# Weight additions and row scaling of a second feed-forward product moved from GpSimd to VectorE

## The chip, the cores and the metric

The kernel runs on one core of a Trainium2 chip. The metric is the device time of one execution in microseconds (us). The core has five engines that each work through their own list of instructions in the order written: TensorE (matrix products; PE in the profile, its weight loads PEld), VectorE (DVE), ScalarE (ACT), GpSimd (POOL) and SyncE (SP), which here only issues transfers. They wait for one another through semaphores.

## The reference

One layer of a decoder for 2048 tokens of width 1024, in fp32. Around the part that matters here:

```python
h = h + jnp.einsum('bsm,md->bsd', mixed, w_out[l])       # after the two mixers
nm = rmsnorm(h, mlp_norm_g[l])
a = jnp.square(jax.nn.relu(jnp.einsum('bsd,df->bsf', nm, w_ff1[l])))   # width 4096
h = h + jnp.einsum('bsf,fd->bsd', a, w_ff2[l])
...
return rmsnorm(h, final_norm_g)
```

The change lies in the last product, `a` (2048 x 4096) by `w_ff2` (4096 x 1024), and in the final norm, which divides each token's row by its root mean square and multiplies it by a vector of 1024 factors.

## The kernel before

Everything is fp32; a product of two fp32 matrices is made of three matmuls on rounded parts. Each operand is split into a high part (a rounded copy, made by ScalarE) and a low part (the operand less its high part, made by VectorE), and `mm3` (L132 to L134) adds high by high, low by high and high by low in PSUM.

The second feed-forward product isn't done block by block. Each half of the tokens (1024) has four blocks of 256 rows, the inner width of 4096 is cut into four, the 1024 output columns into two. Instead of 4 x 4 x 2 = 32 block products a half, the kernel does 26 products of combinations: sums and differences of activation blocks by sums and differences of weight blocks, each result added to or subtracted from some of the eight output sums of a half. The table `PRODUCTS` lists for each product which combination of activations it takes, its sign, whether it begins a new accumulation in PSUM, and which output sums take it (numbered l = 2m + n, row block m and column half n). The combinations of activations were formed and stored to memory during the first feed-forward product. The combinations of weights are formed on the way: three raw buffers of 1024 x 512 (each in two halves of 128x2048) hold them, and the table `WEIGHTS` says for each of 24 weights for how many products it serves, in which buffer it lies, what is loaded into which buffer, and the one addition or subtraction of two buffers that makes it. The lists `first_of` and `weight_of` turn this into product numbers. `tD` is a combination kept in memory.

Time is counted in steps: 26 products, each for two halves (a phase, `ph`), each phase of 8 steps, and in a step six matmuls (one chunk of 128 of the inner width, for two groups of 128 tokens, three matmuls each): 416 steps. The order of every engine's instructions is written out by hand: `at_step(n, f, ...)` puts an instruction into the list of step n, and `step(n)` issues that list, in the order in which it was filled, before the matmuls of step n. What belongs to the change's surroundings, for a weight whose first product begins at step `at`:

- `load_t` (L1664, SP's queue): the raw weight halves, at steps at - 22 and at - 16
- `add_t` (L1672): the addition, a quarter (128x1024) at a time, at steps at - 16, - 13, - 9 and - 6
- `hi_t` (L1684, ScalarE) and `lo_t` (L1688, VectorE): the two parts of each quarter (tile `ct`), between steps at - 11 and at - 1
- for the activations of a phase: `load_s` (L1633, SP), `hi_s` (L1646, ScalarE) and `lo_s` (L1651, or L1653 for a product of negative sign; VectorE; tile `cs`), 6 to 1 steps ahead of their use
- `taken` (L1737, VectorE): in the first two steps behind a phase, adds the finished PSUM results to the output sums (tiles `sum` and `acc`)

When an output sum has its last product, `taken` calls `output` for each group of 128 rows: `square` (ScalarE, L1708) sums the squares of the 512 columns; where the row's other half is already complete, `root` (VectorE L1714 and L163, then the power on GpSimd, L164) makes the row's factor, `scale` multiplies both halves by it and by the final norm's factors `gF`, and `store` (L1722, L1723, SP's queue) writes them. These are 1, 2, 4 and 6 steps behind; for the last sum (half 1, l = 3) they follow at once. Of a row's two column halves, the second (`C[1]`) is scaled by one VectorE instruction (L1718). The first (`C[0]`) is multiplied by `gF` on GpSimd (L1710) as soon as its sum is complete and squared, and later by the row's factor on ScalarE (L1719).

Weights 17 to 23 of the table begin at products 19 to 25, so at steps 304 to 400; all of them but weight 19 (steps 336 to 351) have an addition, which is made within the 16 steps before the weight's first step.

Of the kernel before, what the change touches and what calls it, by code (L numbers as in the profile page):

```python
# [13 lines left out]
AF = mybir.ActivationFunctionType  # L14
OP = mybir.AluOpType
# [91 lines left out]
def emit(tc, a, stop=99):  # L107
    nc = tc.nc
    V, A, G, T, SP = nc.vector, nc.scalar, nc.gpsimd, nc.tensor, nc.sync
# [44 lines left out]
    def stat(n=1):  # L154
        if stat_at[0] + n > 96:
            stat_at[0] = 0
        s = stats[:, stat_at[0]:stat_at[0] + n]
        stat_at[0] += n
        return s

    def rstd_of(ssq, width, n=1, X=V):
        r, r2 = stat(n), stat(n)
        X.tensor_scalar(r, ssq, 1.0 / width, EPS, op0=OP.mult, op1=OP.add)  # L163
        G.tensor_tensor(r2, r, mhalf[:, :n], op=OP.pow)  # L164
        return r2
# [82 lines left out]
    C = {(0, 0): c11, (0, 1): c12, (1, 0): c21, (1, 1): c22}  # L248
# [309 lines left out]

    R, PV = {}, {}

    def square(key, src, junk):
        R[key] = stat()
        A.activation(junk, src, AF.Square, accum_out=R[key])

    def root(key):
        R[key] = rstd_of(R[key], D)

    def scale(key, src, cs=slice(0, D)):
        V.scalar_tensor_tensor(src[:, cs], src[:, cs], R[key], gB[:, cs], op0=OP.mult, op1=OP.mult)

# [21 lines left out]
    def spread_roots(k):  # L592

        rows[k] = ps("d")
        for i in range(4):
            T.matmul(rows[k][:, 128 * i:128 * i + 128], R[8 + 4 * k + i].to_broadcast([128, 128]), ident,
                     start=True, stop=True)
# [146 lines left out]
    with tc.manual_schedule(engines={X.engine for X in (T, V, A, G, SP)}):  # L744
# [79 lines left out]
        for t in range(3, 8):  # L824
            n = t + 1
# [23 lines left out]
        for t in range(12, base[NG] + 10):  # L849
# [7 lines left out]
            if T0 <= t < base[NG]:  # L857
                g = max(g for g in range(NG) if base[g] <= t)
                x, i = divmod(t - base[g], length[g])
# [426 lines left out]
    for pr in range(4):  # L1286
# [3 lines left out]
        for hh, br in seq:  # L1290
            b = Branch()
            b.h, b.br = 2 * pr + hh, br
            m = 4 if br == 2 else 2
# [66 lines left out]
    gM, gF = gs[:, :D], gs[:, D:2 * D]  # L1360
# [215 lines left out]
    for at, t in enumerate(tiles):  # L1576
        u, m = nxt
# [37 lines left out]
    first_of, weight_of = [], []  # L1615
# [39 lines left out]
    def traw(b, h):  # L1655
        if (b, h) not in raw_t:
            raw_t[b, h] = view(acc1[2 + h] if b == 2 else slot("rt"), (4, 512))
        return raw_t[b, h]
# [7 lines left out]
    def add_t(q, u):  # L1666

        _, _, _, add, stored = WEIGHTS[q]
        if add is not None:
            d, x, op, y = add  # L1670
            d, x, y = [traw(b, u // 2)[:, u % 2 * 2:u % 2 * 2 + 2] for b in (d, x, y)]
            G.tensor_tensor(d, x, y, op=OP.add if op == "+" else OP.subtract)  # L1672
            if stored:
                at_step(now[0] + 4, SP.dma_start, tD[:, 2 * u:2 * u + 2], d)

# [21 lines left out]
    def output(half, l, i):  # L1697

        m, n = divmod(l, 2)
        scr = gM[:, 512 * (i % 2):512 * (i % 2) + 512]  # L1700
        C = [sums[half, m][:, i, 512 * k:512 * k + 512] for k in range(2)]
        col = 16 * half + 4 * m + 2 * i
        at_end = last_at[l] > last_at[2 * m + 1 - n]
        row = 1024 * half + 256 * m + i * 128
        R = []

        def square():
            A.activation(scr, C[n], AF.Square, accum_out=oss[:, col + n:col + n + 1])  # L1708
            if n == 0:
                G.tensor_tensor(C[0], C[0], gF[:, :512], op=OP.mult)  # L1710

        def root():
            s1 = stat()
            V.tensor_tensor(s1, oss[:, col:col + 1], oss[:, col + 1:col + 2], op=OP.add)  # L1714
            R.append(rstd_of(s1, D))

        def scale():
            V.scalar_tensor_tensor(C[1], C[1], R[0], gF[:, 512:], op0=OP.mult, op1=OP.mult)  # L1718
            A.activation(C[0], C[0], AF.Copy, scale=R[0])  # L1719

        def store():
            SP.dma_start(out2[row:row + 128, 512:], C[1])  # L1722
            (A if (half, l, i) == (1, 3, 1) else SP).dma_start(out2[row:row + 128, :512], C[0])  # L1723

        for n_, f in zip((1, 2, 4, 6), (square, root, scale, store) if at_end else (square,)):
            if (half, l) == (1, 3):
                f()
            else:
                at_step(now[0] + n_, f)

    def taken(ph, i, p):

        k, half = divmod(ph, 2)
        for l, sign in PRODUCTS[k][3]:
            m, n = divmod(l, 2)
            c = sums[half, m][:, i, 512 * n:512 * n + 512]
            V.tensor_tensor(c, c, p, op=OP.add if sign > 0 else OP.subtract)  # L1737
            if last_at[l] == k:
                output(half, l, i)
# [8 lines left out]
    steps, now = {}, [0]  # L1748
# [8 lines left out]
    def at_step(n, f, *args):  # L1757
        steps.setdefault(n, []).append((f, args))
# [6 lines left out]
    for ph in range(2 * NR):  # L1765
        for u, n in ((0, -6), (1, -3)):
            n = 4 if (ph, u) == (1, 1) else 8 * ph + n
# [4 lines left out]
    for q, at in enumerate(first_of):  # L1772
        at *= 16
        for h, n in ((0, -22), (1, -16)):
            at_step(max(at + n, -4 + 3 * h) if q else -18 + h, load_t, q, h)
        for u in range(4):
            at_step(at + (-16, -13, -9, -6)[u], add_t, q, u)
        for u in range(4):
            n = at + ((-11, -8, -4, -2) if q else (-10, -8, -5, -2))[u]
            at_step(n, hi_t, q, u)  # L1780
            at_step(n + 1, lo_t, q, u)
# [21 lines left out]
    with tc.manual_schedule(engines={X.engine for X in (T, V, A, G, SP)}):  # L1803
# [16 lines left out]
        for at in range(7, len(jobs1)):  # L1820
# [3 lines left out]
            m = parts_at.get(at - 1)  # L1824
# [15 lines left out]
            if at in parts_at:  # L1840
                m = parts_at[at]
# [89 lines left out]
```

## Time and profile before

| what | us |
|---|---|
| median of 3 runs | 2247.17 |
| lowest and highest of them | 2245.4, 2248.27 |
| profiled execution, its own time | 2247.4 |
| its span in the trace | 2245.6 |
| busy: TensorE, VectorE, ScalarE, GpSimd | 2224.3, 1616.8, 1158.0, 846.6 |
| additions of weights (L1672) in the whole stage | 72 instructions on GpSimd |
| products by `gF` (L1710) | 16 instructions on GpSimd |

The span runs from the first to the last recorded instruction; times of rows are counted from its start. A row of the trace in order of time has its start, its length, the engine, the line of the kernel, the instruction, the tiles as out<-in, the shapes, and a count where equal neighbours are merged; in brackets stands how long the engine had been idle and what released it. A row of a group has the count, the busy time, the mean length in ns, and the idle time in front. The table of waits gives the total, the number and the longest. Matmuls overlap, so a matmul's length (0.39 us) is longer than the distance between two starts.

### The profile page before, as it was taken

How to read it: one execution, taken by the hardware profiler on the slowest of the kernel's cores; microseconds unless marked ns; L12 is line 12 of the kernel's file. 1: busy time of each engine (PE TensorE's matmuls, PEld its weight loads, DVE VectorE, ACT ScalarE, POOL GpSimd, SP SyncE). 2: the span in 40 equal slices, each digit the busy share in tenths (PEclk: the TensorE clock that was granted, in tenths of full speed). 3: DMA queues.
4: the chain of work that ended last, by engine and by line, in shares of the span. 5: the costliest groups of instructions: out<-in, count | busy, mean ns of one | idle time of the engine just before them, and what ended most of it. 6: DMA issues, size and time to landing. Idle time of an engine off the chain costs nothing.

```text
span 2245.6 us, 34257 instructions
## 1 busy us (share of the span) xinstructions
PE 2224.3 (99%) x12276; PEld 1921.4 (86%) x12276; DVE 1616.8 (72%) x2743; ACT 1158.0 (52%) x2076; POOL 846.6 (38%) x824
## 2 busy tenths in 40 slices
PE   9999999999999999999999999999999999999998
PEld 7978998899999998888888887888888788888886
DVE  6867867646666783447677779777776878758897
ACT  6564436426777772225555557655562333324544
POOL 2112000115478765300122358232346545242665
PEclk9999999999999999999999999999999999999999
DMA  7268345757767863777454567454588553454563
GB/s 208 88 212 255 123 138 175 252 170 236 225 198 248 265 227 130 226 244 256 116 155 135 153 190 220 144 154 141 155 281 300 184 174 127 140 169 152 175 217 113
DMA packets 312618, 419.42 MB, mean 187 GB/s; under 512 B 20917, under 2 KB 237534, under 8 KB 307712
## 3 DMA queue, kind: packets, MB, share of 16 engines
q1 hardware_dynamic: 312302, 416.97, 58.6%
q8 instruction: 96, 1.57, 0.3%
q14 instruction: 74, 0.61, 0.1%
q10 hardware_dynamic: 146, 0.27, 0.0%
HBM read 272.68 MB, written 149.20 MB: 188 GB/s over the span
## 4 chain that ended last, share of the span: by engine, by line
PE 88%; DVE 6%; issue 2%; DMA 2%; ACT 1%; POOL 0%; SPq 0%; POOLq 0%; DVEq 0%; ACTq 0%
PE ps_a L132 10%; PE ps_a L134 10%; PE ps_a L133 10%; PE ps_c L132 8%; PE ps_c L133 8%; PE ps_c L134 8%; PE ps_a L1017 5%; PE ps_d L134 4%; PE ps_d L132 4%; PE ps_d L133 4%; PE ps_d L998 3%; PE ps_c L978 2%; PE ps_c L976 2%; DVE ct L1688 2%; PE ps_o L132 2%
## 5 line engine op out<-in xcount | busy, mean ns | idle before, releaser
L1466 ACT ACTIVATE w1comb<-w1raw 128x512 fp32r<-128x512 f32 x224 | 141.1, 632 | 222.0 <-PE ps_a L134 76.1
L1646 ACT ACTIVATE cs<-rs 128x1024 fp32r<-128x1024 f32 x104 | 109.7, 1055 | 223.1 <-PE ps_c L134 132.2
L1471 DVE TENSOR_TENSOR w1comb<-w1raw,w1comb 128x512 fp32r<-128x512 f32 x224 | 188.3, 843 | 24.7 <-ACT w1comb L1466 24.6
L989 ACT ACTIVATE pe<-pe,O 128x256 f32<-128x256 f32 (+1 forms) x384 | 156.0, 454 | 63.0 <-DVE O L988 57.5
L1017 PE MATMUL ps_a<-v,pt 128*128 128x65 f32 x1200 | 180.3, 253 | 0.0
L1017 PEld LDWEIGHTS ps_a<-v,pt 128*128 128x128 f32 x1200 | 174.7, 194 | 0.9
L998 PE MATMUL ps_d<-ident,pe 128*128 128x128 f32 x600 | 158.9, 279 | 0.0
L988 DVE CUSTOM_DVE_ANT_0 pe<-ps_c,nb 128x256 f32<-128x256 f32 (+1 forms) x384 | 126.6, 361 | 42.1 <-PE ps_d L998 16.6
L1688 DVE TENSOR_TENSOR ct<-rt,ct 128x1024 fp32r<-128x1024 f32 x68 | 134.7, 1981 | 18.6 <-ACT ct L1684 18.6
L132 PE MATMUL ps_a<-hb,w1comb 128*128 128x512 f32 x376 | 146.5, 390 | 0.4 <-ACT xt L1514 0.4
L133 PE MATMUL ps_a<-hb,w1comb 128*128 128x512 f32 x376 | 146.4, 389 | 0.0
L134 PE MATMUL ps_a<-hb,w1comb 128*128 128x512 f32 x376 | 146.3, 389 | 0.0
L132 PE MATMUL ps_c<-ct,cs 128*128 128x512 f32 x360 | 140.1, 389 | 0.0
L134 PE MATMUL ps_c<-ct,cs 128*128 128x512 f32 x360 | 140.1, 389 | 0.0
L133 PE MATMUL ps_c<-ct,cs 128*128 128x512 f32 x360 | 140.1, 389 | 0.0
L164 POOL TENSOR_TENSOR stats<-stats,mhalf 128x1 f32<-128x1 f32 (+1 forms) x64 | 47.6, 745 | 241.5 <-DVE stats L163 241.5
L930 POOL CAST qp<-qs 128x512 fp32r<-128x512 f32 x64 | 66.9, 1128 | 190.2 <-DVE wraw L306 174.3
L1569 POOL TENSOR_TENSOR acc<-acc 128x256 f32<-128x256 f32 x83 | 84.3, 1027 | 139.3 <-DVE acc L1569 126.4
L294 ACT ACTIVATE wcomb<-wraw 128x512 fp32r<-128x512 f32 (+2 forms) x119 | 88.9, 754 | 61.7 <-DVE wraw L306 25.0
L1653 DVE SCALAR_TENSOR_TENSOR cs<-rs,cs 128x1024 fp32r<-128x1024 f32 (+1 forms) x56 | 97.7, 1751 | 30.8 <-ACT cs L1646 30.5
L998 PEld LDWEIGHTS ps_d<-ident,pe 128*128 128x128 f32 x600 | 108.8, 186 | 0.3
L1569 POOL TENSOR_TENSOR xt<-acc,acc 128x256 f32<-128x256 f32 x32 | 28.6, 893 | 211.9 <-ACT acc L1533 189.7
(444 smaller groups left out, 7325.1 us busy)
## 6 DMA issues: line engine op xcount, KB each, us to landing
rs<-actD SPq DMA_DIRECT2D x103, 512.0 KB, 4.3
actD<-acc SPq DMA_DIRECT2D x288, 128.0 KB, 2.9
w1raw<-w_ff SPq DMA_DIRECT2D x32, 1024.0 KB, 7.3
rt<-w_ff SPq DMA_DIRECT2D x24, 1024.0 KB, 7.4
k<-kD SPq DMA_DIRECT2D x16, 1024.0 KB, 8.8
wraw<-w_in SPq DMA_DIRECT2D x12, 1024.0 KB, 6.8
cmb<-boD SPq DMA_DIRECT2D x16, 528.0 KB, 6.6
wraw<-w_in SPq DMA_DIRECT2D x16, 512.0 KB, 5.1
```

The lines of the kernel that those rows point to most:

```text
L132: T.matmul(out, sh, mh, start=first, stop=False, skip_group_check=more)
L133: T.matmul(out, sl, mh, start=False, stop=False, skip_group_check=more)
L134: T.matmul(out, sh, ml, start=False, stop=last, skip_group_check=more)
L988: V.tensor_tensor_reduce(p, s, bias, scale=1.0, scalar=BIG, op0=OP.add, op1=OP.min, accum_out=nm)
L989: A.activation(p, p, AF.Exp, bias=nm, scale=-1.0)
L998: T.transpose(pb[:, i * 128:i * 128 + 128], src, ident)
L1017: T.matmul(self.b.opsum[:, n % 4], self.pt[:, i * 128:i * 128 + 128], self.b.v[:, blk, cols], start=first, stop=last)
L1466: A.activation(c[:, 0], v, AF.Copy)
L1471: V.tensor_tensor(c[:, 1], v, c[:, 0].bitcast(F32), op=OP.subtract)
L1569: (G if pool or all_pool[0] else V).tensor_tensor(t[l], t[x], t[y], op=OP.add if op == "+" else OP.subtract)
L1646: A.activation(v[:, 0], x, AF.Copy, scale=float(PRODUCTS[ph // 2][2]))
L1688: V.tensor_tensor(v[:, 1], x, v[:, 0].bitcast(F32), op=OP.subtract)
```

## The change

Two things in this stage go from GpSimd to VectorE. First, the additions of weights: those of every weight whose first product is number 19 or later (`first_of[q] > 18`, weights 17 to 23, six of which have an addition, 24 instructions) are issued to VectorE's list at the same steps. The additions of the weights before stay on GpSimd. Second, the finished rows: the product of `C[0]` with `gF` is no longer made on GpSimd. For 14 of the 16 groups of rows, `scale` multiplies `C[0]` by the row's factor and by `gF` in one VectorE instruction, as it does `C[1]`, and the copy on ScalarE is gone. For the two groups of half 1, m = 1, whose column halves are complete last, the product by `gF` is kept ahead but put on VectorE, 32 steps later than before, and ScalarE's copy stays. GpSimd keeps the powers of `root`.

```diff
@@ add_t
-            G.tensor_tensor(d, x, y, op=OP.add if op == "+" else OP.subtract)
+            (V if first_of[q] > 18 else G).tensor_tensor(d, x, y, op=OP.add if op == "+" else OP.subtract)
@@ output
+        ahead = half == m == 1
 
         def square():
             A.activation(scr, C[n], AF.Square, accum_out=oss[:, col + n:col + n + 1])
-            if n == 0:
-                G.tensor_tensor(C[0], C[0], gF[:, :512], op=OP.mult)
+            if n == 0 and ahead:
+                at_step(now[0] + 32, lambda: V.tensor_tensor(C[0], C[0], gF[:, :512], op=OP.mult))
...
         def scale():
             V.scalar_tensor_tensor(C[1], C[1], R[0], gF[:, 512:], op0=OP.mult, op1=OP.mult)
-            A.activation(C[0], C[0], AF.Copy, scale=R[0])
+            if ahead:
+                A.activation(C[0], C[0], AF.Copy, scale=R[0])
+            else:
+                V.scalar_tensor_tensor(C[0], C[0], R[0], gF[:, :512], op0=OP.mult, op1=OP.mult)
```

## The prediction

> **What bounds the kernel now.** I read the page first, then the table of busy times for the stretch the change touches, then VectorE's own rows there in order of time, then who waited for whom. The page:
>
> ```profile
> span 2245.6 us, 34257 instructions
> PE 2224.3 (99%) x12276; PEld 1921.4 (86%) x12276; DVE 1616.8 (72%) x2743; ACT 1158.0 (52%) x2076; POOL 846.6 (38%) x824
> ```
>
> TensorE is the bound over the whole program; an edit on VectorE can give back only what TensorE waits for VectorE. Neither share tells that for this stage. The stretch of the 24 additions and its last quarter, by engine, and then the additions' line alone:
>
> ```profile
> 2058.00:2218.00 160.00, 156.64 (x686) 127.91 (x685) 146.08 (x122) 77.77 (x116) 111.95 (x50) 1.00 0.54 175
> ...
> 2178.70:2218.00 39.30, 35.94 (x153) 27.92 (x153) 37.52 (x25) 18.41 (x29) 35.26 (x15) 1.00 0.25 83
> ```
> ```profile
> 2058.00:2218.00 160.00, 72.70 (x24) 1.00 0.54 175
> ```
>
> Columns: length, then busy us (count) of PE, PEld, VectorE, ScalarE, GpSimd (in the last row GpSimd's 24 additions alone), granted clock 1.00, DMA. VectorE is busy 146.1 of 160 us, 37.5 of the last 39.3; 72.7 of GpSimd's 112.0 us are the additions. How far it is behind TensorE shows in its rows in order of time:
>
> ```profile
> 2055.90 1.23 DVE L1651 TENSOR_TENSOR cs<-rs,cs 128x1024 fp32r<-128x1024 f32 x1
> 2057.04 1.23 DVE L1688 TENSOR_TENSOR ct<-acc,ct 128x1024 fp32r<-128x1024 f32 x1
> 2058.59 0.69 DVE L1737 TENSOR_TENSOR sum<-sum,ps_c 128x512 f32<-128x512 f32 x1 [0.33 <-PE ps_c L134]
> ...
> 2091.23 1.28 DVE L1737 TENSOR_TENSOR sum<-sum,ps_a 128x512 f32<-128x512 f32 x2 [1.30 <-PE ps_a L134]
> ...
> 2139.48 0.67 DVE L1737 TENSOR_TENSOR sum<-sum,ps_a 128x512 f32<-128x512 f32 x1
> ...
> 2163.10 0.68 DVE L1737 TENSOR_TENSOR acc<-acc,ps_a 128x512 f32<-128x512 f32 x1
> ...
> 2176.00 0.67 DVE L1737 TENSOR_TENSOR acc<-acc,ps_d 128x512 f32<-128x512 f32 x1
> ...
> 2199.93 0.68 DVE L1737 TENSOR_TENSOR sum<-sum,ps_d 128x512 f32<-128x512 f32 x1
> ...
> 2234.27 0.69 DVE L1737 TENSOR_TENSOR acc<-acc,ps_d 128x512 f32<-128x512 f32 x1 [1.55 <-PE ps_d L134]
> ```
>
> L1737 adds a finished partial product to its sum; in the written order the first one of half a product stands at a step that is a multiple of 8, and a step is six matmuls. The two early rows wait for TensorE, so they date it: steps 288 and 312 lie 24 x 6 = 144 matmuls and 32.64 us apart, 0.2267 us a matmul, 1.36 us a step. With TensorE never stopped, step s would be at 2091.23 + 1.36(s - 312). VectorE's rows of steps 344, 360, 368 and 384 are then 4.7, 6.6, 8.6 and 10.8 us late: it falls behind steadily. From the row at 2091.23 to the last one quoted TensorE has 609 matmuls (of 2496 in the stage, 1869 lie before the first and 18 behind the last): 138.0 us at its pace, and 143.0 were taken. **TensorE lost 5.0 us.** Where:
>
> ```profile
> 2180.00 0.50 PE L133 MATMUL ps_d<-ct,cs 128*128 128x512 f32 x1 [0.86 <-DVE cs L1653]
> ```
> ```profile
> PE ps_d L133 <- DVE cs L1653: 1.9, 2, 1.0
> PE ps_a L133 <- DVE cs L1651: 1.4, 1, 1.4
> ```
>
> The first stop comes only after VectorE is 8.6 us behind; all three listed waits (3.3 of the 5.0 us; the rest is the refill behind each and stops under half a microsecond) are for L1651/L1653, VectorE's low halves of the activations. And why VectorE is behind:
>
> ```profile
> 2206.04 3.41 DVE L1688 TENSOR_TENSOR ct<-rt,ct 128x1024 fp32r<-128x1024 f32 x1
> ...
> 2217.53 1.22 DVE L1688 TENSOR_TENSOR ct<-rt,ct 128x1024 fp32r<-128x1024 f32 x1
> ```
> ```profile
> 2127.29 2.40 POOL L1672 TENSOR_TENSOR acc<-rt 128x1024 f32<-128x1024 f32 x1
> ...
> 2205.00 10.07 POOL L1672 TENSOR_TENSOR rt<-rt,acc 128x1024 f32<-128x1024 f32 x3
> ```
>
> The same VectorE instruction takes 3.41 us while GpSimd runs an addition, and 1.22 us once GpSimd has ended (2205.00 + 10.07 = 2215.07). GpSimd's own addition goes from 2.40 to 10.07 / 3 = 3.36. A pair that runs at once costs VectorE 3.41; both done by VectorE cost 2.44.
>
> **The change part by part.** (1) 24 additions of 128x1024 (six weights, four quarters) go from GpSimd to VectorE. No such line on VectorE before; the nearest row is L1688, also 128x1024, two fp32 SBUF inputs: 24 x 1.22 = 29.3 us. From above it is bounded by the contended 3.41 (81.8), which needs a partner on GpSimd, and GpSimd keeps only 128x1 powers. I take 1.22.
> (2) 14 finished half rows are scaled by one VectorE instruction of L1718's kind in place of a GpSimd product and a ScalarE copy; the two of half 1, rows 256 to 511 keep the copy, and their product comes 32 steps later, on VectorE:
>
> ```profile
> L1688 DVE TENSOR_TENSOR ct<-acc,ct 128x1024 fp32r<-128x1024 f32 x17 | 34.3, 2018 | 1.0 <-ACT ct L1684 0.9
> L1651 DVE TENSOR_TENSOR cs<-rs,cs 128x1024 fp32r<-128x1024 f32 x18 | 31.8, 1768 | 5.9 <-ACT cs L1646 5.8
> L1688 DVE TENSOR_TENSOR ct<-rt,ct 128x1024 fp32r<-128x1024 f32 x12 | 29.4, 2448 | 0.5 <-ACT ct L1684 0.5
> L1653 DVE SCALAR_TENSOR_TENSOR cs<-rs,cs 128x1024 fp32r<-128x1024 f32 x12 | 24.5, 2041 | 3.2 <-ACT cs L1646 3.0
> L1718 DVE SCALAR_TENSOR_TENSOR sum<-sum,stats,gs 128x512 f32<-128x512 f32 x12 | 11.1, 927 | 1.9 <-POOL stats L164 1.9
> L1714 DVE TENSOR_TENSOR stats<-oss 128x1 f32<-128x1 f32 x16 | 4.1, 255 | 3.2 <-ACT gs L1708 3.2
> L1718 DVE SCALAR_TENSOR_TENSOR acc<-acc,stats,gs 128x512 f32<-128x512 f32 x4 | 2.9, 750 | 1.4 <-POOL stats L164 1.3
> L163 DVE TENSOR_SCALAR stats<-stats 128x1 f32<-128x1 f32 x16 | 2.5, 154 | 0.6
> ```
>
> (VectorE's groups from 2058 on; last column: idle before them.) 16 x 0.75 = 12.0 us more on VectorE, the two late products priced like the scalings. So 41.3 us are added.
> (3) What VectorE gets back: the 59 operations of 128x1024 take 120.0 us; at 1.22 each, 72.0: 48.0 less. The 12 scalings at 0.927 become 0.75: 2.1; the 16 sums of statistics at 0.255 become 0.154: 1.6. Together 51.7. **Net VectorE has 10.4 us less to do**, 135.7 of a stretch that can shrink to 155.
> (4) Is that enough in each part? The room is 16 steps = 21.8 us per product. Back to back a 128x1024 operation costs 1.14 (the starts 2055.90 and 2057.04), an L1737 half of 1.28, a scaling about 0.7. Steps 336 to 352 are the fullest: eight low halves 9.1, four additions 4.6, four accumulations 2.6, four rows of two scalings and two small ones 4 x 1.7 = 6.8: 23.1 us, 1.3 over the room. Before it lies a weight without an addition (9.1 + six accumulations 3.8 + two rows 3.4 = 16.3), behind it 20, 16 and 20. Waits on ScalarE and GpSimd inside a period, by the idle time of today (13.9 us in 160), add 1.9. The lag peaks near 3 us, where 8.6 did not yet stop TensorE.
> (5) A new wait: an addition in VectorE's order now waits for its weight block to land, and the low halves (TensorE's stops) and the accumulations queue behind it. Blocks are fetched 7 steps (9.5 us) ahead of their addition:
>
> ```profile
> 2150.97 0.39 SPq L1664 DMA_DIRECT2D rt<-tD  x1
> ...
> 2173.18 0.39 SPq L1664 DMA_DIRECT2D rt<-w_ff  x1
> ```
> ```profile
> rt<-w_ff SPq DMA_DIRECT2D x6, 1024.0 KB, 7.5
> ```
> ```profile
> 2158.24 2.71 POOL L1672 TENSOR_TENSOR acc<-rt,acc 128x1024 f32<-128x1024 f32 x1 [0.33 <-DMA rt<-tD]
> ```
>
> Step 359, where VectorE would add the first of these, is at 2155.2: the block landed 3.1 us too late; for the second, 2173.18 + 7.5 = 2180.7 against step 375 at 2176.9: 3.8. But on SP's queue both stand behind loads that wait for L1653 and stores that wait for L1718, and those stood on VectorE, which was 4.7 to 8.6 us late there. With 3 us of lag the blocks come about 2 to 5 us sooner and the wait is 0 to 1. SP also waits for two scalings a row in place of one: 0.7 more per row. Even unchanged, 3.8 is inside 8.6. I take nothing on the path; bounds 0 and, both in a row, 6.9 + 3 - 8.6 = 1.3.
> (6) Nothing more: 14 fewer ScalarE copies beside 78 busy us of 160 are hidden work gone; the powers no longer queue behind additions, which only shortens a row that is not last. At the end:
>
> ```profile
> 2231.30 1.42 DVE L1718 SCALAR_TENSOR_TENSOR acc<-acc,stats,gs 128x512 f32<-128x512 f32 x2
> ...
> 2240.89 0.75 DVE L1718 SCALAR_TENSOR_TENSOR acc<-acc,stats,gs 128x512 f32<-128x512 f32 x1 [0.66 <-POOL stats L164]
> ```
>
> The rows at 2231.30 get two scalings more, ending near 2231.30 + 2.84 = 2234.14, just before VectorE is wanted at 2234.27; the last row, 2240.89 on, keeps its copy and its chain, up to the end at 2245.6. The two late products (1.4 us) fall in steps 401 and 402, where no addition is left; without that cover they would cost 1.4.
> **Sum:** the stops of 5.0 us go, and I leave 0.2 for new small ones (between the 0 and 1.3 of part 5): 4.8. The profiled execution took 2247.4 us for its span of 2245.6, so 2242.6 for one like it; it lay 0.2 over the median of 2247.17, and so the median comes to **2242.4 us**.
>
> **The rivals.** *Late weight blocks* (B): the two scalings per row delay SP further, and the blocks of steps 359 and 375 land 2 us later than today: 6.9 + 4 + 3 - 8.6 = 5.3 at worst, 1.3 at best, taken together about 2.5 of the gain: 2245. For it: the rows above; against: SP waits for a VectorE that is faster.
> *The stops are not VectorE's* (C): its lateness follows from SP's loads and ScalarE, and the change does not do what it should: 2247.2. Against: every listed stop names VectorE, whose rows from 2204 to 2213 follow each other without idle time.
> *Slower* (D): VectorE's long durations are not GpSimd's doing but stay. Then 41.3 us come on top of an engine with 13.9 idle in 160: 27.4 more, 2274. It decides at 27.4 us of the 51.7 expected back: with less than half of them returned, the additions cost TensorE more than it lost before. Against: 3.41 and 1.22 of the same instruction 11 us apart. The Trainium skill, Perfetto Trace Analysis, "Optimizing Scalar/DVE Operations", says that work may be moved off a saturated VectorE to ScalarE or even GpSimd; by that this change goes the wrong way, and the time would be D's. The same section warns that the two share an SBUF read port, so that moving work between them may not help; the pair of 3.41 and 3.36 agrees with the warning.
>
> **How the numbers follow.** Forecast 0.80, B 0.08, C 0.06, D 0.06. About 0.2% (4.5 us, to 2242.7) is what a measurement of this kernel can tell from no change, and the forecast is just beyond it: its own range, 2241.2 to 2243.6, is cut by that line, some 0.62 on the faster side. Faster 0.50, within 0.2% 0.30 + 0.08 + 0.06 = 0.44, slower 0.06. The range reaches from 2241.0 over B to 2246.0.
>
> **What would show it.** Right: L1688's group at 1.22 mean from 2058 on, the additions on VectorE near 1.22, no row of TensorE waiting for L1651 or L1653, accumulations of steps 344 to 384 within 3 us of TensorE, the last wait for ps_d near 2229.3. Wrong: VectorE waiting long for a weight block (B), L1688 still above 2 us (D), the same three stops with a VectorE that has idle time in front of them (C).

## The result

The changed kernel takes 2242.03 us (median of 15 runs, 2240.35 to 2245.31), the kernel before, in the same comparison, 2246.72 us (15 runs, 2244.66 to 2248.37). The ratio is 0.998 with a 95% interval of 0.9974 to 0.9987: 4.7 us less, and the predicted 2242.4 is 0.4 us off.

The profile after, first the page, then the busy times of the two stretches shown of before (columns as there):

```profile
span 2241.8 us, 34217 instructions
PE 2222.9 (99%) x12276; PEld 1921.5 (86%) x12276; DVE 1614.3 (72%) x2783; ACT 1148.5 (51%) x2062; POOL 741.8 (33%) x784
```
```profile
2058.00:2218.00 160.00, 160.00 (x707) 132.48 (x707) 137.92 (x171) 75.67 (x113) 11.07 (x12) 1.00 0.56 183
2178.70:2218.00 39.30, 39.30 (x175) 32.56 (x174) 33.41 (x44) 18.34 (x29) 4.00 (x4) 1.00 0.27 91
```

TensorE is busy for all of the 160 us, where it had been busy for 156.6, and gets 707 matmuls into them in place of 686. VectorE has 49 more instructions there and is busy 8.2 us less. GpSimd has 11.1 us left, the powers. VectorE's groups from 2058 on show why:

```profile
L1651 DVE TENSOR_TENSOR cs<-rs,cs 128x1024 fp32r<-128x1024 f32 x19 | 23.2, 1221 | 8.9 <-ACT cs L1646 8.9
L1688 DVE TENSOR_TENSOR ct<-acc,ct 128x1024 fp32r<-128x1024 f32 x17 | 20.7, 1217 | 0.0
L1653 DVE SCALAR_TENSOR_TENSOR cs<-rs,cs 128x1024 fp32r<-128x1024 f32 x12 | 14.7, 1222 | 8.1 <-ACT cs L1646 8.1
L1688 DVE TENSOR_TENSOR ct<-rt,ct 128x1024 fp32r<-128x1024 f32 x12 | 14.6, 1217 | 0.0
...
L1672 DVE TENSOR_TENSOR acc<-rt,acc 128x1024 f32<-128x1024 f32 x8 | 9.7, 1218 | 0.0
...
L1723 DVE SCALAR_TENSOR_TENSOR sum<-sum,stats,gs 128x512 f32<-128x512 f32 x12 | 8.9, 744 | 0.0
```

Every 128x1024 operation takes 1.22 us, the additions (L1672) among them; L1688 had 2.0 and 2.4, L1653 2.0. The new scalings (L1723) take 0.744. VectorE now waits in front of L1651 and L1653 for ScalarE (17.0 us), so it is no longer behind with them most of the time. The accumulations, now on L1741, in order of time:

```profile
2092.47 1.28 DVE L1741 TENSOR_TENSOR sum<-sum,ps_a 128x512 f32<-128x512 f32 x2 [0.17 <-PE ps_a L134]
...
2103.35 1.28 DVE L1741 TENSOR_TENSOR sum<-sum,ps_d 128x512 f32<-128x512 f32 x2 [1.30 <-PE ps_d L134]
...
2136.77 0.68 DVE L1741 TENSOR_TENSOR sum<-sum,ps_a 128x512 f32<-128x512 f32 x1
...
2160.44 0.68 DVE L1741 TENSOR_TENSOR acc<-acc,ps_a 128x512 f32<-128x512 f32 x1
...
2169.59 0.68 DVE L1741 TENSOR_TENSOR acc<-acc,ps_d 128x512 f32<-128x512 f32 x1
...
2190.39 0.69 DVE L1741 TENSOR_TENSOR sum<-sum,ps_d 128x512 f32<-128x512 f32 x1 [0.17 <-PE ps_d L134]
...
2230.51 0.69 DVE L1741 TENSOR_TENSOR acc<-acc,ps_d 128x512 f32<-128x512 f32 x1 [2.19 <-PE ps_d L134]
```

From 2092.47 to 2230.51 are 138.04 us for the same 609 matmuls, which took 143.04 before and need 138.0 at TensorE's pace: all 5.0 us of stops are gone. Counted from the row at 2103.35 (step 320), the rows of steps 344, 360, 368 and 384 are 0.8, 2.7, 1.0 and 0 us late (before: 4.7, 6.6, 8.6, 10.8).

The two spans differ by 3.8 us only, because this execution came to step 280, where nothing that moved has run yet, 1.24 us later than the one profiled before (L1741 at 2048.95, L1737 at 2047.71) and was still 1.24 later at step 312. The medians, over 15 runs each, show 4.7. The waits of TensorE for low halves that the table of waits still lists for this stage lie at 1731 and 1760, beside additions that stayed on GpSimd:

```profile
PE ps_a L133 <- DVE cs L1653: 0.9, 1, 0.9
...
PE ps_a L133 <- DVE cs L1651: 0.5, 1, 0.5
```

### The profile page after: what moved, and what is told of

The parts are those of the page before. It is cut to its first block, busy times and chain, and to the rows that moved or that the text cites. A ratio compares the mean times of both kernels' runs of the same rounds, so it can differ in the third digit from the quotient of the medians.

```text
span 2241.8 us, 34217 instructions
## 1 busy us (share of the span) xinstructions
PE 2222.9 (99%) x12276; PEld 1921.5 (86%) x12276; DVE 1614.3 (72%) x2783; ACT 1148.5 (51%) x2062; POOL 741.8 (33%) x784
## 4 chain that ended last, share of the span: by engine, by line
PE 91%; DVE 3%; DMA 3%; issue 1%; ACT 1%; POOL 0%; SPq 0%; POOLq 0%; DVEq 0%; ACTq 0%
PE ps_a L132 10%; PE ps_a L134 10%; PE ps_a L133 10%; PE ps_c L132 9%; PE ps_c L133 9%; PE ps_c L134 9%; PE ps_a L1017 5%; PE ps_d L134 4%; PE ps_d L133 4%; PE ps_d L132 4%; PE ps_d L998 3%; PE ps_c L978 2%; PE ps_c L976 2%; PE ps_o L132 2%; PE ps_o L134 2%; PE ps_o L133 2%
## 5 line engine op out<-in xcount | busy, mean ns | idle before, releaser
L1688 DVE TENSOR_TENSOR ct<-rt,ct 128x1024 fp32r<-128x1024 f32 x68 | 125.6, 1847 | 15.8 <-ACT ct L1684 15.7
L1653 DVE SCALAR_TENSOR_TENSOR cs<-rs,cs 128x1024 fp32r<-128x1024 f32 (+1 forms) x56 | 87.5, 1569 | 31.7 <-ACT cs L1646 31.7
L133 PE MATMUL ps_c<-hb,w1comb 128*128 128x512 f32 x264 | 103.0, 390 | 1.3 <-DVE w1comb L1471 1.3
```

The costliest lines, as they stand in the source:

```text
L133: T.matmul(out, sl, mh, start=False, stop=False, skip_group_check=more)
L1688: V.tensor_tensor(v[:, 1], x, v[:, 0].bitcast(F32), op=OP.subtract)
```

## The experiments

The theory: TensorE stops when VectorE is more than about 8 us behind; VectorE is behind because GpSimd's two-input additions and its own two-input operations hold each other up; on VectorE alone both fit. The rivals: the scaling of the rows is what counts; GpSimd's results came late, and the long durations are no cause; VectorE has room to spare anyway; waiting in order for weight blocks eats the gain.

**The additions alone.** `scale` and `square` as before:

```diff
-            G.tensor_tensor(d, x, y, op=OP.add if op == "+" else OP.subtract)
+            (V if first_of[q] > 18 else G).tensor_tensor(d, x, y, op=OP.add if op == "+" else OP.subtract)
```

> Only the 24 additions go to VectorE; the products by gF stay on GpSimd and the copies on ScalarE. Theory (lateness of VectorE beyond about 8.6 us is what stops TensorE, and GpSimd's additions cause most of it): VectorE no longer falls behind, the stops of 5.0 us go, the time is that of the whole change, 2242 (2241 to 2243.5); L1688 still has a few rows above 2 us, next to GpSimd's 16 products. Rival (the finished rows' scaling is what counts): 2246 or more, stops still there.

Measured: 2241.23 us, ratio 0.998 (0.9971 to 0.9989). No stop of TensorE after 1765 in its trace. The additions alone give the whole gain. GpSimd's 16 products still show in VectorE's groups from 2058 to 2218, at means between 1.22 and 1.62 (single rows of L1688 beside a product take up to 2.32, as expected):

```profile
L1651 DVE TENSOR_TENSOR cs<-rs,cs 128x1024 fp32r<-128x1024 f32 x18 | 25.6, 1422 | 8.5 <-ACT cs L1646 8.3
...
L1672 DVE TENSOR_TENSOR rt<-rt 128x1024 f32<-128x1024 f32 x4 | 6.5, 1616 | 0.0
```

**The scaling alone.** The changed kernel with all additions on GpSimd:

```diff
-            (V if first_of[q] > 18 else G).tensor_tensor(d, x, y, op=OP.add if op == "+" else OP.subtract)
+            G.tensor_tensor(d, x, y, op=OP.add if op == "+" else OP.subtract)
```

> Only the scaling of finished rows goes to VectorE; the 24 additions stay on GpSimd. Theory: the additions still stretch VectorE's rows to 3.4 us; by the sums per 16 steps the lag still grows, by about 5 us in steps 336 to 352 and 1.6 in 352 to 368 and 384 to 400, to about 7.6 us, close to the 8.6 at which TensorE first stopped: 0 to 2 us of stops are left, 2242 to 2245. Rival (the scalings alone load VectorE more than GpSimd's products cost it): 5 us of stops or more, 2247 and above.

Measured: 2242.86 us, ratio 0.9987 (0.9978 to 0.9996); here too TensorE has no stop after 1765. VectorE's accumulations in this run:

```profile
2113.74 0.69 DVE L1741 TENSOR_TENSOR sum<-sum,ps_a 128x512 f32<-128x512 f32 x1 [1.31 <-PE ps_a L134]
...
2173.84 0.68 DVE L1741 TENSOR_TENSOR acc<-acc,ps_d 128x512 f32<-128x512 f32 x1
...
2196.88 0.67 DVE L1741 TENSOR_TENSOR sum<-sum,ps_d 128x512 f32<-128x512 f32 x1
```

From step 328 at 2113.74, steps 368 and 384 are due at 2168.1 and 2189.9: the lag is 5.7 and 7.0 us, against 7.6 worked out beforehand, and 7.0 us of lag stop nothing. So the two parts don't add up: each brings VectorE under the limit, and what is left under it costs no time. The written order gives the limit its size: a low half stands five steps ahead of the matmuls that read it (the first of a phase) or six (the second), 6.8 or 8.2 us at TensorE's pace. That the whole is faster than this part is not told apart by the intervals.

**GpSimd busy again, for nothing.** VectorE's list is that of the changed kernel; GpSimd adds the same two blocks behind it, into a tile nobody reads:

```diff
             (V if first_of[q] > 18 else G).tensor_tensor(d, x, y, op=OP.add if op == "+" else OP.subtract)
+            if first_of[q] > 18:
+                G.tensor_tensor(view(xt, (2, 512)), d, y, op=OP.add)
```

> The whole change, and GpSimd makes, for each of the 24 additions, one addition of the same size behind VectorE's, whose result nobody uses (the output is the same). VectorE's own list is the same as in the changed kernel. Theory (two engines that read at once stretch each other): VectorE's 128x1024 rows beside GpSimd's are 3.4 us again, its lag grows by about 6 us per 16 steps, to about 18; less the 8.6 of slack some 9 us of stops (5 to 12): 2251 (2247 to 2254). Rival (the change helps because GpSimd's results were late, not because the engines slow each other): 2242, no stops, L1688 at 1.22.

Measured: 2254.65 us, ratio 1.0041 (1.0027 to 1.0054): 12.6 us over the changed kernel's 2242.03, which was measured in another comparison; by the two ratios it is 0.6%, near 14 us. The rows of VectorE, of GpSimd and of TensorE around one of the stops, and VectorE's groups:

```profile
2167.87 2.60 DVE L1690 TENSOR_TENSOR ct<-acc,ct 128x1024 fp32r<-128x1024 f32 x1
```
```profile
2167.50 1.89 POOL L1674 TENSOR_TENSOR xt<-acc 128x1024 f32<-128x1024 f32 x1 [5.13 <-DVE acc L1672]
```
```profile
2173.40 0.50 PE L133 MATMUL ps_a<-ct,cs 128*128 128x512 f32 x1 [2.52 <-DVE cs L1653]
...
2222.58 0.80 PE L133 MATMUL ps_a<-ct,cs 128*128 128x512 f32 x1 [3.75 <-DVE cs L1651]
```
```profile
L1690 DVE TENSOR_TENSOR ct<-acc,ct 128x1024 fp32r<-128x1024 f32 x16 | 32.4, 2028 | 0.0
L1690 DVE TENSOR_TENSOR ct<-rt,ct 128x1024 fp32r<-128x1024 f32 x12 | 25.0, 2083 | 0.0
```

L1690 is the line of L1688 in this kernel: 2.03 and 2.08 us on average in place of 1.22. The 3.4 us that were expected show in single rows only (up to 3.44). Nothing waits for these additions of GpSimd, so late results are not the cause. (The tiles they read are held a little longer, but from 2058 on no row of VectorE waits for a transfer, and VectorE waits 2.0 us for GpSimd's powers, as in the changed kernel.) The first stop, at 2146.80, shows that 8 us of lag is no sharp limit: the accumulation before it (2137.66, step 344, counted from a row at 2047.19 that waited for TensorE at step 280) is 3.4 us late, but the low half that TensorE waits for then takes 3.44 itself. The loss is at the upper end of what was expected, a little over it: 13.0 us lost by TensorE, not 9, of which some 3 are matmuls at a slower pace behind the two longest stops (last section).

**GpSimd busy without reading.** The same, with a fill:

```diff
             (V if first_of[q] > 18 else G).tensor_tensor(d, x, y, op=OP.add if op == "+" else OP.subtract)
+            if first_of[q] > 18:
+                G.memset(xt, 0.0)
```

> The changed kernel, and GpSimd fills a 128x1024 tile with a constant 24 times (it writes and reads nothing; nobody uses it). Theory (what slows both is that both read; so the Trainium skill, SBUF - State Buffer, Who interferes with whom): L1688 stays at 1.22 beside it, no stops, 2242. Rival (any work of GpSimd slows VectorE): L1688 above 1.5 on average, stops, 2245 or more.

Measured: 2242.24 us, ratio 0.9979 (0.9969 to 0.9988). With nothing to wait for, the fills ran in bursts; ten of them lie beside these rows of VectorE:

```profile
2151.02 10.08 POOL L1674 MEMSET xt<- 128x1024 f32 x10
```
```profile
2153.70 1.22 DVE L1690 TENSOR_TENSOR ct<-acc,ct 128x1024 fp32r<-128x1024 f32 x1
...
2160.57 1.22 DVE L1690 TENSOR_TENSOR ct<-acc,ct 128x1024 fp32r<-128x1024 f32 x1
```

1.22 us, as alone; the twelve VectorE operations of 128x1024 from 2058 on that lie beside a fill take 1.22 to 1.23. It isn't GpSimd's being at work that slows VectorE but what its additions do and its fills don't: read. The Trainium skill, SBUF — State Buffer, "Who interferes with whom", says that a VectorE instruction with two SBUF inputs contends with a GpSimd instruction that reads SBUF and not with one that only writes; these rows agree.

**VectorE's room.** Each of the 24 additions made twice on VectorE, the second into a tile nobody reads:

```diff
             (V if first_of[q] > 18 else G).tensor_tensor(d, x, y, op=OP.add if op == "+" else OP.subtract)
+            if first_of[q] > 18:
+                V.tensor_tensor(view(xt, (2, 512)), d, y, op=OP.add)
```

> The changed kernel, and VectorE makes each of the 24 additions a second time into a tile nobody reads (the output is the same): 24 x 1.14 = 27.4 us more on VectorE, nothing on GpSimd. Theory: by the sums per 16 steps VectorE is then 5.9 us over in steps 336 to 352, 2.5 in 352 to 368, 1 under in 368 to 384, 2.4 over in 384 to 400, with waits inside the periods a lag of some 10 to 15 us; what is over the slack of about 8.6 stops TensorE: 2247 (2244 to 2251). Rival (VectorE has room to spare here, its own work was never the limit): 2242.

Measured: 2250.22 us, ratio 1.0016 (1.0007 to 1.0025). Of 27.4 us more work 8.0 reach the end. No operation is longer than before (L1690 1.218 in its trace), TensorE stops four times between 2156 and 2174. VectorE's last accumulation that waits for TensorE and the one ahead of the first stop, then the first stop and the longest:

```profile
2047.16 0.69 DVE L1743 TENSOR_TENSOR sum<-sum,ps_a 128x512 f32<-128x512 f32 x1 [1.31 <-PE ps_a L134]
...
2153.89 0.68 DVE L1743 TENSOR_TENSOR sum<-sum,ps_c 128x512 f32<-128x512 f32 x1
```
```profile
2157.65 0.50 PE L133 MATMUL ps_d<-ct,cs 128*128 128x512 f32 x1 [0.77 <-DVE cs L1653]
...
2173.47 0.50 PE L133 MATMUL ps_a<-ct,cs 128*128 128x512 f32 x1 [3.00 <-DVE cs L1653]
```

From step 280 at 2047.16, step 352 is due at 2145.1: TensorE first stops when VectorE is 8.8 us late, close to the 8.6 of before, and here without any long operation. So VectorE has a limit after the change as well: its lag reaches 2.7 us of the 8 or so that cost nothing.

**All additions on VectorE.** The stops left at 1731 to 1760 asked for it:

```diff
-            (V if first_of[q] > 18 else G).tensor_tensor(d, x, y, op=OP.add if op == "+" else OP.subtract)
+            V.tensor_tensor(d, x, y, op=OP.add if op == "+" else OP.subtract)
```

> The whole change, and the additions of the earlier weights on VectorE too; GpSimd adds no weights at all. Theory: the changed kernel still has stops of about 2.8 us at 1731 to 1764, before low halves on VectorE that run beside GpSimd's additions; they go as well: 2239.2 (2238 to 2241). Rival (VectorE, in its own order, now waits for weight blocks that land late, as GpSimd did there, 2 to 11 us at a time): new stops of TensorE before 2058, 2242 or more.

Measured: 2247.16 us, ratio 1.0006 (0.9997 to 1.0014): the gain of the change is gone, and the rival was right. The first weight that is added (weight 2) is loaded into a tile (`acc`) that the first feed-forward product uses up to its end. VectorE's row of that addition and TensorE's rows around the stop:

```profile
1719.50 1.23 DVE L1672 TENSOR_TENSOR rt<-acc,rt 128x1024 f32<-128x1024 f32 x1 [14.95 <-DMA acc<-w_ff]
```
```profile
1718.32 0.39 PE L132 MATMUL ps_c<-ct,cs 128*128 128x512 f32 x1
1725.50 0.79 PE L133 MATMUL ps_c<-ct,cs 128*128 128x512 f32 x1 [6.79 <-DVE cs L1651]
1726.09 0.63 PE L134 MATMUL ps_c<-ct,cs 128*128 128x512 f32 x1
1726.52 0.63 PE L132 MATMUL ps_o<-ct,cs 128*128 128x512 f32 x1
```

VectorE stood 14.95 us; TensorE stopped for 6.79, so some 8 us were absorbed. Behind it this run has no stop at all. The prediction's late weight blocks (B) are real, only not at the weights that the change moves.

**All but the first.** Weight 2's additions back on GpSimd:

```diff
-            (V if first_of[q] > 18 else G).tensor_tensor(d, x, y, op=OP.add if op == "+" else OP.subtract)
+            (V if first_of[q] > 3 else G).tensor_tensor(d, x, y, op=OP.add if op == "+" else OP.subtract)
```

> The changed kernel, with the additions of all earlier weights on VectorE too, except the first one (weight 2), whose block landed 15 us after VectorE got to it. Theory: the stops at 1728 to 1764 that come of GpSimd's additions of weights 3 to 5 go; the one near 1731 beside weight 2's may stay (up to 1.2 us); VectorE waits up to 5 us for weight 3's block, which the slack takes: 1.5 to 2.5 us less than the changed kernel, 2240 (2238 to 2241.5). Rival (weight 3's block is late by more than the slack too): a stop of several us before 1760, 2242 or more.

> The changed kernel itself, to stand beside the next one on the same chip: 2242, within 0.1% of its earlier ratio 0.998.

Measured, on one chip: 2240.24 us, ratio 0.997 (0.9958 to 0.9981), beside the changed kernel's 2242.21, ratio 0.998 (0.9971 to 0.9989). One stop is left in its trace from 1640 on, beside weight 2's additions:

```profile
1732.38 0.50 PE L133 MATMUL ps_a<-ct,cs 128*128 128x512 f32 x1 [0.72 <-DVE cs L1651]
```

**The first one later.** All additions on VectorE, weight 2's later in its order:

```diff
-            at_step(at + (-16, -13, -9, -6)[u], add_t, q, u)
+            at_step(at + ((-11, -9, -7, -5) if q == 2 else (-16, -13, -9, -6))[u], add_t, q, u)
```

> All additions of weights on VectorE, as in the run with all of them, but those of the first weight (weight 2) stand 5 steps or less later in the order (at - 11, - 9, - 7 and - 5 in place of - 16, - 13, - 9 and - 6), so that VectorE reaches them about when the block lands. Theory (the wait of 15 us was the whole loss of that run): it shrinks to some 3 to 8 us, which the slack of about 8 us takes; no GpSimd addition is left to slow anything, no stop of 0.3 us or more from 1640 on: 2239.3 (2238 to 2241). Rival (the block lands later when VectorE's order decides): a stop of several us near 1725, 2242 or more.

> The kernel that keeps only weight 2's additions on GpSimd, once more, beside the one before on the same chip: 2240.2, ratio 0.997 (0.996 to 0.998).

Measured, on one chip: 2240.51 us, ratio 0.9969 (0.9957 to 0.9981), and 2240.62, ratio 0.9965 (0.9953 to 0.9978), for the run with weight 2 on GpSimd. VectorE waits 8.6 us in two pieces, and TensorE stops once, against the expectation of no stop, though the time is in the range:

```profile
1722.01 1.23 DVE L1672 TENSOR_TENSOR rt<-acc,rt 128x1024 f32<-128x1024 f32 x1 [6.61 <-DMA acc<-w_ff]
...
1729.85 1.23 DVE L1672 TENSOR_TENSOR rt<-acc,rt 128x1024 f32<-128x1024 f32 x1 [2.00 <-DMA acc<-w_ff]
```
```profile
1734.00 0.50 PE L133 MATMUL ps_a<-ct,cs 128*128 128x512 f32 x1 [0.78 <-DVE cs L1651]
```

The two are the same time. Both lie about 7 us under the kernel before and about 2 under the change; against the change the intervals overlap, but the run beside it on one chip was 2.0 us faster, and the two later ones agree with that. No faster version than these two was found.

## Why the prediction was right

- *TensorE lost 5.0 us, to VectorE's low halves.* Right: the same 609 matmuls took 138.04 us after, with no row of TensorE waiting for L1651 or L1653 in the stretch.
- *An addition costs 1.22 us on VectorE, the others come back to 1.22* (parts 1 and 3). Right: 1.214 to 1.218 for the additions, 1.217 to 1.222 for the rest. VectorE's busy time from 2058 to the end fell from 162.0 to 149.1 us, 13 where 10.4 had been worked out. Busy time counts rows that overlap once, though; added up by lengths the rows fell from 169.3 to 159.8 us, with one low half (1.2 us) more inside the window, so by 10.7 us for the same work. The late products took 0.68 where 0.75 was put in.
- *The lag peaks near 3 us* (part 4). Right: 2.7 at step 360.
- *No weight block comes late* (part 5). Right, and for the reason given: SP's queue went faster, because the loads and stores in front waited for a VectorE that was on time (SP's listed waits from 2100 to 2182 are all for VectorE, 69.2 us before and 62.0 after). The second halves that were 3.1 and 3.8 us late were issued here at

```profile
2149.51 0.47 SPq L1664 DMA_DIRECT2D rt<-tD  x1
...
2167.80 0.43 SPq L1664 DMA_DIRECT2D rt<-w_ff  x1
```

1.5 and 5.4 us sooner than before, 2.7 and 6.6 against the 1.24 us later clock of this execution (2 to 5 had been said, so the second gained more), and no row of VectorE in the stretch waits for a transfer. The 0.2 us left for new small stops were not needed.
- *The end is unchanged* (part 6). Right: from the last wait for ps_d to the end of the span are 11.3 us, as before (2230.51 to 2241.8; 2234.27 to 2245.6). That wait had been put near 2229.3; less the 1.24 us it is 2229.27.
- *About 0.2% is what a measurement can tell from no change.* Too cautious: with 15 runs each the interval is 0.13% wide (below 1 by 0.13 to 0.26%), and the 4.7 us are clear of no change.
- *The rivals.* B did not happen here, but it did at weight 2. C (VectorE is not what stops TensorE) and D (the long durations are not GpSimd's doing) are shown wrong: GpSimd's unused additions bring the long durations and the stops back, and the doubled work on VectorE alone brings stops without long durations.
- What the prediction didn't say: that either part would have been enough. The sum "5.0 us of stops go" has no shares; 7.0 us of lag cost as little as 2.7. It also left open whether VectorE's 3.41 us are a slower operation or a wait; the rows in the last section show a wait.

## What to carry to other kernels

Before moving work between two engines, look for the same instruction at two lengths in the trace: a second engine that holds it up for longer than the moved work would take makes the move lighten even the busier engine. In this case an engine beside the bound cost nothing until its lag passed the slack, and beyond it roughly what was over; so find the slack in the trace (the lag at the first stop) and work out the lag period by period, not the busy share. And an instruction moved into another engine's order brings its waits with it: check when its inputs land at the earliest place, not at a typical one.

## What the hardware showed

VectorE and GpSimd took turns here rather than both running slower. In the run with GpSimd's unused additions GpSimd's row shown above ends at 2169.39 and VectorE's beside it at 2170.47, 1.08 us later; so it is with the rows of 3.12 (2138.25) and 3.44 us (2143.30), beside additions of 2.41 that began at 2137.88 and 2143.25. VectorE's operation was held until the addition that had begun first was done, and then took about its usual time. What has one input in PSUM was not held. VectorE's rows of the kernel before, beside GpSimd's additions from 2205.00 to 2215.07:

```profile
2209.37 0.68 DVE L1737 TENSOR_TENSOR sum<-sum,ps_a 128x512 f32<-128x512 f32 x1
...
2212.73 0.67 DVE L1737 TENSOR_TENSOR sum<-sum,ps_c 128x512 f32<-128x512 f32 x1
2213.33 1.76 DVE L1714 TENSOR_TENSOR stats<-oss 128x1 f32<-128x1 f32 x1
```

The accumulations take their 0.68; the sum of 128x1 with two inputs in SBUF, 0.15 us alone, lasts until the addition ends.

Behind a long stop TensorE has a stretch at a slower pace. After the stop of 6.79 us twelve matmuls follow at 0.43 us in place of 0.2267 (the row 1726.52 above is the first of them), after stops of 2.5 to 3.8 us five to seven, not always from the first matmul on; after stops of up to 1.4 us only the next matmul is late, at 0.34. The busy times of the run with the 6.79 us stop over 1724 to 1734, columns as above, have a granted clock of 0.64:

```profile
1724.00:1734.00 10.00, 8.50 (x25) 6.75 (x26) 10.00 (x11) 3.25 (x4) 0.00 (x0) 0.64 0.74 263
```

Counted in gaps between matmul starts, the waits of 2.52, 3.00 and 3.75 us cost 4.4, 5.0 and 5.4. The Trainium skill, TensorE: Matmul & The Clock Gate, Part 1, gives 426.7 ns between matmuls of 512 columns on the slow clock, and about 3.4 us of idleness before it; the spacing agrees, and here 2.5 us of waiting for the low half (2.9 between the starts) were already enough.

The stops at 1728 to 1768 come and go between executions of the same code: summed over gaps between matmul starts they are 2.8 us in the profile of the change, 2.5 in its second one, 1.4 and 3.3 in those of the two parts, none in that with the fills. What decides it is open; it is within the spread between runs of one kernel (5 us). Another part of that spread lies far ahead of the stage: from 835 to 850 the granted clock is 0.89 in the profile of the change and 1.00 in those of the additions alone and of the fills, the two fastest profiled executions here.
